# Sums of squares of the head norms in portions between column tiles, and another order of three branch products

## The chip, the cores and the metric

One core of a Trainium2 chip runs the whole program. The metric is the device time of one execution in microseconds (us). A median of several runs is compared; lower is better.

## What is computed

Two transformer blocks over 256 tokens of width 1024, in float32. Block one mixes a stick-breaking attention and a gated linear attention, then a feed-forward. Block two, where the change lies, is cut here to what matters:

```python
xn = rms_norm_2(x, norm_mix)
q_nsa, kv_nsa, g_nsa, conv_in, q_mem, g_merge = split(xn @ w_in)
q  = rms_norm_2(heads(q_nsa), qk_norm[0])              # 8 heads of 64
kc = rms_norm_2(compress_blocks(k_c, ...), qk_norm[1]) # gelu(blocks @ w1) @ w2
ks, kw = rms_norm_2(k_s, qk_norm[2]), rms_norm_2(k_w, qk_norm[3])   # 2 groups of 64
o_nsa  = nsa_attention(q, kc, vc, ks, vs, kw, vw, sigmoid(g_nsa))   # sparse attention
u      = silu(layer_norm(causal_conv(a * sigmoid(ag))))
qm     = rms_norm_2(q_mem, mem_qk_norm[0])             # 4 heads of 128
o_m    = softmax(qm @ km^T / sqrt(128)) @ vm           # attention to the memory
gm     = sigmoid(g_merge)                              # three gates of width 1024
merged = gm[0] * (o_nsa @ w_nsa_out) + gm[1] * (u @ w_conv_out) + gm[2] * (o_m @ w_mem_out)
h      = x + merged @ w_out
```

A feed-forward with a gate follows. The change alters no formula; only the order of the three terms of `merged` in their sum is another.

## The kernel before

Activations lie transposed: features on the 128 partitions, tokens along the row. Each weight matrix streams in as tiles of 128x1024 float32 (512 KB) on the queue of SP. `Stream.prepare` (L505 to L522) loads a tile into one of four `raw` buffers, casts it on ACT into one of three `hi` buffers (L520) and subtracts on DVE into one of three `lo` buffers (L522). A float32 product is made of three: hi times xh, hi times xl, lo times xh. In `gemm_b` these are L324, L326 and L328, eight matmuls of 128x256 each per column tile of 128 columns when the inner dimension is 1024; the first pair of column tiles of a matrix can run in an interleaved order, L308 to L310 (lead). `gemm_a` (L367) puts the tokens on the partitions instead.

In `block_two` a section written out by hand (from L1095, `manual_schedule` for TensorE alone) sets TensorE's order. ACT's, DVE's and POOL's orders come from a scheduler, which goes by the priorities and by the place where an instruction is written. Generators hand out the work: `heads` makes the column tiles of the queries and keys, `cmp` is `compress` (eight small products "chunks" L1229 that gather a block's frames, a fold L1239, a gelu, then L1258, L1266, L1272), `gates` makes the 24 column tiles of the merge gates, and `pre` is `nsa_operands`. Each `next` issues one step of a generator, and `fill(g, n)` issues n column tiles.

`nsa_operands` squares the keys `ksw`, the queries `q` and the memory's queries `qm` on ACT (L1310, tile `hsq`), and sums the squares over each head on TensorE with the 20 matmuls of L1313, in which the squares are the weights (128x128) and the right side has one or two columns. Each is two passes in the trace, so 40 instructions. DVE adds an epsilon (`hn_v`, L1319), `rsqrt_exp` (L1292 to L1296) makes the reciprocal root in ACT and DVE, and L1328 spreads the keys' norms. Here it is called at once, behind the fold L1239; L1117 (a small product for the head gates) and `gemm_a` (the values, L367) come next, and then L1258, which needs the gelu's result `cmp_h` (L1250). The sigmoid of the gelu is `cmp_t`: L1283 (DVE), L1284 (ACT), L1285 and L1286 (DVE).

Beyond the hand-written section TensorE's order is the scheduler's too. `branch(n)` multiplies a product by its gate (L1151, DVE) and adds into a running sum (L1153): `wmo` (memory) starts the sum, `wno` (sparse attention) is added on POOL, `wco` (convolution) on DVE; then `split` (ACT L426, DVE L427) makes the halves `mrg` that `wo2` reads first in its lead loop L308. In `before`, `wmo` comes first, while the last head of the memory attention (L1520) is still being made.

Of the kernel before, what the change touches and what calls it, by code (L numbers as in the profile page):

```python
# [13 lines left out]
OP = mybir.AluOpType  # L14
# [423 lines left out]
def fill(steps, n):  # L438
    for _ in range(n):
        next(steps, None)  # L440


def finish(steps):
    for _ in steps:
        pass
# [597 lines left out]
def block_two(K, B, KM, vm, out):  # L1043
    nc, tc, a, par, con = K.nc, K.tc, K.a, K.par, K.con
# [5 lines left out]
    ON, OM = Halves(K, "on", 4), Halves(K, "om", 4)  # L1050
    gm = [K.t4("gm") for _ in range(6)]
    cv = K.t4("cv")
    kc2 = [K.small("PT", [128, 384], bufs=4)[:, :256].rearrange("p (g t) -> p g t", g=2) for _ in range(2)]
    N = Bag()
# [43 lines left out]
    with tc.manual_schedule(engines={mybir.EngineType.PE}):  # L1098
        heads = K.steps_b(_Shift(st, 64), 8, 12, B.X, evb)
        fill(heads, 6)  # L1100
        cmp = compress(K, kc2, N)
        for _ in range(6):
            next(cmp)
            fill(heads, 1)
        next(cmp)
        pn = K.gemm_n(K.narrow("wgn", B.gain), B.x)
        with tc.high_priority(offset=50000):
            nc.vector.tensor_tensor(gn, pn, rr, op=OP.mult)
        next(cmp)
        gates = K.steps_b(K.stream("w2g"), 8, 24, B.X, evg)  # L1110
        fill(gates, 2)
        next(cmp)
        pre = nsa_operands(K, N, B.eps)
        next(pre)
        pg = K.pt()[:, :48].rearrange("p (t n) -> p t n", t=2)
        for t in range(2):
            mm(pg[:, t], lhsT=gn[:, t * 128:t * 128 + 128], rhs=con["fold"][:, :24], start=True, stop=True)  # L1117
        N.gate = K.small("gate", [128, 2, 24], bufs=1)
        with tc.issue_after(s3.ins):
            nc.scalar.preload_act_table_set("natural_log_exp_and_others")  # L1120
            sigmoid(K, N.gate, pg)

        K.gemm_a(K.stream("w2v", 256), 8, 1, B.X, 256, evv)
        next(cmp)
        finish(pre)
        fill(gates, 1)
        finish(cmp)
        with tc.issue_after(s3.ins):
            last = nsa(K, N, ON, mem_attention(K, N, KM, vm, OM), gates)
        finish(gates)  # L1130
# [16 lines left out]
    def branch(n):  # L1147
        def ev(i, c, ps):
            d = slice((i % 4) * 256, (i % 4 + c) * 256)
            g_, t = gm[2 * n + i // 4][:, d], gm[4 + i // 4][:, d]  # L1150
            nc.vector.tensor_tensor(g_, ps.rearrange("p a t -> p (a t)"), g_, op=OP.mult)  # L1151
            if n != 2:
                (nc.vector if n == 1 else nc.gpsimd).tensor_tensor(t, t, g_, op=OP.add)  # L1153
            if n == 1:
                K.split(M.h(i, c), M.l(i, c), t)
        return ev

    K.gemm_b(K.stream("wmo"), 4, 8, OM, branch(2))
    K.gemm_b(K.stream("wno"), 4, 8, ON, branch(0))
    K.gemm_b(K.stream("wco"), 4, 8, UC, branch(1), single=2)  # L1160
    XF = Halves(K, "xf", 8)
    sqs = Squares(K)
# [118 lines left out]
def sigmoid(K, out, x, scale=1.0):  # L1281

    K.nc.vector.tensor_scalar(out, x, -87.0 / scale, None, op0=OP.max)  # L1283
    K.nc.scalar.activation(out, out, AF.Exp, scale=-scale)  # L1284
    K.nc.vector.tensor_scalar(out, out, 1.0, None, op0=OP.add)  # L1285
    K.nc.vector.reciprocal(out, out)  # L1286


def rsqrt_exp(K, v, y, t):

    nc = K.nc
    nc.scalar.activation(t, v, AF.Ln)  # L1292
    nc.scalar.activation(y, t, AF.Exp, scale=-0.5)
    nc.vector.tensor_tensor(t, y, y, op=OP.mult)
    nc.vector.scalar_tensor_tensor(t, t, -0.5, v, op0=OP.mult, op1=OP.mult)
    nc.vector.scalar_tensor_tensor(y, t, 1.5, y, op0=OP.add, op1=OP.mult)  # L1296
    return y


def nsa_operands(K, N, eps):  # L1300

    nc, par, con = K.nc, K.par, K.con
    mm = nc.tensor.matmul
    q, ksw = N.q, N.ksw
    sums = K.pt()[:, :32].rearrange("p (t n) -> p t n", t=2)
    at = 0
    for x, n, rhs, m in ((ksw, 2, con["mean64"][:, ::64], 2), (q, 4, con["mean64"][:, ::64], 2),
                         (N.qm, 4, con["one128"], 1)):
        sq = K.t4("hsq")[:, :n * 256]
        nc.scalar.activation(sq, x, AF.Square)  # L1310
        for t in range(2):
            for i in range(n):
                mm(sums[:, t, at + i * m:at + i * m + m], lhsT=sq[:, i * 256 + t * 128:i * 256 + t * 128 + 128],  # L1313
                   rhs=rhs, start=True, stop=True)
        at += n * m
    v, y, w = (K.small(n, [128, 32], bufs=1) for n in ("hn_v", "hn_y", "hn_w"))
    y3 = y.rearrange("p (t n) -> p t n", t=2)
    for t in range(2):
        nc.vector.tensor_scalar(v[:, t * 16:t * 16 + 16], sums[:, t], eps[:, t:t + 1], None, op0=OP.add)  # L1319
    rsqrt_exp(K, v, y, w)  # L1320
    rk, N.rq, N.rqm = y3[:, :, :4], y3[:, :, 4:12], y3[:, :, 12:]
    yield
    pk = K.pt()
    for j in range(2):
        for g in range(2):
            for t in range(2):
                o = j * 256 + t * 128
                mm(pk[g * 64:g * 64 + 64, o:o + 128], lhsT=rk[:, t, 2 * j + g:2 * j + g + 1].to_broadcast([128, 64]),  # L1328
                   rhs=K.ident, start=True, stop=True)
    KK = ksw.rearrange("p (j t) -> p j t", j=2)  # L1330
    for j in range(2):
        nc.vector.scalar_tensor_tensor(KK[:, j], ksw[:, j * 256:j * 256 + 256], K.gain_k[:, 1 + j:2 + j],
                                       pk[:, j * 256:j * 256 + 256], op0=OP.mult, op1=OP.mult)


    N.qs = [K.t4("qs", F32R) for _ in range(2)]
    N.kh, N.kl = (K.t4("ks", F32R).rearrange("p (g n) -> p g n", g=2) for _ in range(2))
    for g in range(2):
        own, far = slice(g * 64, g * 64 + 64), slice(64 - g * 64, 128 - g * 64)
        nc.scalar.copy(N.qs[g][own], q[own])  # L1340
        nc.vector.tensor_tensor(N.qs[g][far], q[own], N.qs[g][own].bitcast(F32), op=OP.subtract)
        nc.scalar.copy(N.kh[own, g], ksw[own])
        nc.vector.tensor_tensor(N.kl[own, g], ksw[own], N.kh[own, g].bitcast(F32), op=OP.subtract)
        nc.scalar.copy(N.kh[far, g], ksw[own])
        nc.scalar.copy(N.kl[far, g], N.kl[own, g].bitcast(F32))
# [144 lines left out]
def mem_attention(K, N, KM, vm, OM):  # L1490
    nc = K.nc
    mm = nc.tensor.matmul
    qm, rq = N.qm, N.rqm

    def head(h):
        hs = slice(h * 256, h * 256 + 256)
        ps = K.pt().rearrange("p (t m) -> p t m", t=2)
        for t in range(2):
            mm(ps[:, t], lhsT=qm[:, h * 256 + t * 128:h * 256 + t * 128 + 128], rhs=KM[:, hs], start=True, stop=True)
        mx, den = K.small("mxm", [128, 2], bufs=2), K.small("denm", [128, 2], bufs=2)  # L1500
        nc.vector.tensor_reduce(mx, ps, axis=mybir.AxisListType.X, op=OP.max)
        nc.vector.scalar_tensor_tensor(mx, mx, -1.0, rq[:, :, h], op0=OP.mult, op1=OP.mult)
        P = K.small("P1", [128, 2, 256], bufs=4)
        for t in range(2):
            N.last = nc.scalar.activation(P[:, t], ps[:, t], AF.Exp, scale=rq[:, t, h:h + 1], bias=mx[:, t:t + 1],
                                          accum_out=den[:, t:t + 1])
        nc.vector.reciprocal(den, den)
        for t in range(2):
            nc.vector.tensor_scalar(P[:, t], P[:, t], den[:, t:t + 1], None, op0=OP.mult)
        yield  # L1510
        pt = K.pt().rearrange("p (m t) -> p m t", m=2)
        for t in range(2):
            for m in range(2):
                nc.tensor.transpose(pt[:, m, t * 128:t * 128 + 128], P[:, t, m * 128:m * 128 + 128], K.ident)
        PT = K.small("PTm", [128, 512], bufs=1).rearrange("p (m t) -> p m t", m=2)
        nc.scalar.copy(PT, pt)
        yield
        po = K.pt("pc")[:, :256]
        for m in range(2):
            mm(po, lhsT=vm[:, m * 512 + h * 128:m * 512 + h * 128 + 128], rhs=PT[:, m], start=m == 0, stop=m == 1)  # L1520
        K.split(OM.h(h), OM.l(h), po)

    return head
# [84 lines left out]
```

## Time and profile before

| what | value |
|---|---|
| runs, us | 918.21, 918.55, 919.99 (median 918.55) |
| profiled execution, us | 920.02, of which the trace's span 918.2 |
| TensorE matmul (PE) | 900.6 us busy, 98% of the span |
| TensorE weight loads (PEld) | 828.4 us, 90% |
| DVE | 675.6 us, 74% |
| ACT | 491.1 us, 53% |
| POOL | 51.1 us, 6% |
| mean granted TensorE clock | 0.991 of full |

Busy time counts an instruction from its start to its modelled end; weight loads run beside matmuls. In the trace's views of one engine in order of time, a row merges consecutive instructions of one line: its start, its length, their number, and in brackets the idle time before it with the engine and line that ended it. The next row can start a little before the end of the one ahead, since matmuls are pipelined. In a view of stretches a row has the stretch, its length, the busy time (with the number of instructions) of PE, PEld, DVE, ACT and POOL or of the engine asked for, then the granted TensorE clock (1.00 is 2.4 GHz, 0.50 is 1.2 GHz), the DMA engines' share and GB/s.

### The profile page before, as it was taken

To read this page: it belongs to the slowest core of one execution; us is meant where nothing else is said; L and a number is where in the kernel's file an instruction comes from. 1 tells how busy PE (TensorE), PEld (TensorE's weight loads), DVE (VectorE), ACT (ScalarE), POOL (GpSimd) and SP (SyncE) were. 2 spreads that over 40 slices of the span, in tenths; PEclk is the share of its full clock that TensorE was granted. 3 is DMA by queue.
4 is the path that set the end of the run, shared out by engine and by line. 5 is a ranking of instruction groups with operands and counts; after the bars stand their busy time and mean duration, and the time that the engine had idled before them with its cause. 6 is when DMAs were issued, how large, how long until landed. Compare 5 with 4: busy or idle time off the path is not lost.

```text
span 918.2 us, 17035 instructions
## 1 busy us (share of the span) xinstructions
PE 900.6 (98%) x6818; PEld 828.4 (90%) x6818; DVE 675.6 (74%) x1169; ACT 491.1 (53%) x747; POOL 51.1 (6%) x82
## 2 busy tenths in 40 slices
PE   8998999999999999999999999899999999999998
PEld 6987689999999999888899988799999988888887
DVE  6996768866677666555557986899988788888653
ACT  6653764654456555444444434667854565555432
POOL 1000001210020000001120000000003200000000
PEclk9999999999999999999999998999999999999999
DMA  7643426765666666555656762343445566666672
GB/s 274 202 138 117 115 70 184 228 196 174 195 194 196 180 185 186 173 173 185 189 165 186 225 224 75 95 136 118 116 135 164 184 189 186 191 189 185 193 204 64
DMA packets 45727, 155.64 MB, mean 170 GB/s; under 512 B 5200, under 2 KB 6736, under 8 KB 45648
## 3 DMA queue, kind: packets, MB, share of 16 engines
q1 hardware_dynamic: 45216, 153.48, 54.7%
q8 instruction: 53, 0.87, 0.4%
q10 hardware_dynamic: 432, 1.08, 0.4%
q14 instruction: 26, 0.21, 0.1%
HBM read 153.49 MB, written 1.05 MB: 168 GB/s over the span
## 4 chain that ended last, share of the span: by engine, by line
PE 94%; DVE 3%; issue 1%; ACT 1%; DMA 0%; SPq 0%; DVEq 0%
PE pj L295 18%; PE pj L324 17%; PE pj L326 16%; PE pj L328 16%; PE pj L296 9%; PE pj L367 6%; DVE lo L522 1%; PE pj L309 1%; PE pj L310 1%; PE pj L308 1%; ACT hi L520 1%; PE pt L913 1%; PE pt L1313 1%; PE pt L403 1%; PE pt L1229 1%
## 5 line engine op out<-in xcount | busy, mean ns | idle before, releaser
L520 ACT CAST hi<-raw 128x1024 fp32r<-128x1024 f32 (+1 forms) x278 | 288.6, 1041 | 315.7 <-PE pj L326 133.7
L522 DVE TENSOR_TENSOR lo<-raw,hi 128x1024 fp32r<-128x1024 f32 (+1 forms) x278 | 341.3, 1230 | 105.4 <-ACT hi L520 93.4
L295 PE MATMUL pj<-hid,hi 128*128 128x512 f32 x378 | 134.3, 400 | 0.0
L295 PE MATMUL pj<-xf,hi 128*128 128x512 f32 x320 | 113.2, 399 | 0.0
L296 PE MATMUL pj<-hid,lo 128*128 128x256 f32 x378 | 106.2, 281 | 0.0
L296 PE MATMUL pj<-xf,lo 128*128 128x256 f32 x320 | 89.8, 281 | 0.0
L295 PEld LDWEIGHTS pj<-hid,hi 128*128 128x128 f32 x378 | 71.0, 188 | 17.4
L295 PEld LDWEIGHTS pj<-xf,hi 128*128 128x128 f32 x320 | 60.1, 188 | 14.9
L296 PEld LDWEIGHTS pj<-hid,lo 128*128 128x128 f32 x378 | 71.4, 189 | 0.0
L296 PEld LDWEIGHTS pj<-xf,lo 128*128 128x128 f32 x320 | 60.4, 189 | 0.0
L1536 DVE SCALAR_TENSOR_TENSOR cv<-u,par,cv 128x256 f32<-128x256 f32 x120 | 53.2, 479 | 0.7
L324 PE MATMUL pj<-xm,hi 128*128 128x256 f32 x336 | 50.9, 294 | 0.0
L324 PEld LDWEIGHTS pj<-xm,hi 128*128 128x128 f32 x336 | 44.2, 193 | 5.0 <-ACT hi L520 2.5
L326 PE MATMUL pj<-xm,hi 128*128 128x256 f32 x336 | 47.9, 286 | 0.0
L328 PE MATMUL pj<-xm,lo 128*128 128x256 f32 x336 | 47.2, 283 | 0.0
L328 PE MATMUL pj<-xn,lo 128*128 128x256 f32 x304 | 44.8, 286 | 0.0
L469 POOL TENSOR_TENSOR acc<-acc,ffr 128x256 f32<-128x256 f32 (+1 forms) x25 | 27.3, 1103 | 310.4 <-ACT ffr L462 288.9
L326 PEld LDWEIGHTS pj<-xm,hi 128*128 128x128 f32 x336 | 44.1, 195 | 0.0
L326 PE MATMUL pj<-xn,hi 128*128 128x256 f32 x304 | 44.0, 285 | 0.0
L324 PE MATMUL pj<-xn,hi 128*128 128x256 f32 x304 | 43.8, 285 | 0.0
L328 PEld LDWEIGHTS pj<-xm,lo 128*128 128x128 f32 x336 | 43.5, 193 | 0.0
L328 PEld LDWEIGHTS pj<-xn,lo 128*128 128x128 f32 x304 | 39.7, 192 | 0.5 <-issue 0.4
(471 smaller groups left out, 1632.0 us busy)
## 6 DMA issues: line engine op xcount, KB each, us to landing
raw<-in_wf_dram SPq DMA_DIRECT2D x64, 512.0 KB, 3.7
raw<-in_wgu_dram SPq DMA_DIRECT2D x44, 512.0 KB, 3.7
raw<-in_w1g_dram SPq DMA_DIRECT2D x24, 512.0 KB, 3.8
raw<-in_w2g_dram SPq DMA_DIRECT2D x24, 512.0 KB, 3.7
raw<-in_wdn_dram SPq DMA_DIRECT2D x22, 512.0 KB, 3.9
raw<-in_w2a_dram SPq DMA_DIRECT2D x20, 512.0 KB, 3.7
raw<-in_wo_dram SPq DMA_DIRECT2D x16, 512.0 KB, 3.8
raw<-in_w1a_dram SPq DMA_DIRECT2D x14, 512.0 KB, 3.8
```

Source lines behind the costliest of these rows:

```text
L295: mm(ps, lhsT=st.hi(w), rhs=x.both(k), start=k == 0, stop=False, skip_group_check=True)
L296: mm(ps[:, :T], lhsT=st.lo(w), rhs=x.h(k), start=False, stop=k == kt - 1, skip_group_check=True)
L308: mm(ps[:, j], lhsT=st.hi(w), rhs=x.h(k), start=k + j == 0, stop=False, skip_group_check=True)
L309: mm(ps[:, j], lhsT=st.hi(w), rhs=x.l(k), start=False, stop=False, skip_group_check=True)
L324: mm(ps[:, j], lhsT=st.hi(o + k), rhs=x.h(k), start=k == 0, stop=False)
L326: mm(ps[:, j], lhsT=st.hi(o + k), rhs=x.l(k), start=False, stop=False)
L328: mm(ps[:, j], lhsT=st.lo(o + k), rhs=x.h(k), start=False, stop=k == kt - 1)
L367: mm(pss[t], lhsT=xx(k)[:, t * 128:t * 128 + 128], rhs=ww(o + k), start=k == 0 and xx == x.h and ww == st.hi, stop=k == kt - 1 and ww == s ...
L469: self.engine.tensor_tensor(a, a, s, op=OP.add)
L520: nc.scalar.copy(hi[:, o:o + n], raw[:, o:o + n])
L522: nc.vector.tensor_tensor(lo[:, o:o + n], raw[:, o:o + n], hi[:, o:o + n].bitcast(F32), op=OP.subtract)
L1536: nc.vector.scalar_tensor_tensor(o, u[:, c, k:k + 256], w[:, c, k:k + 1], o, op0=OP.mult, op1=OP.add)
```

## The change

Sums of squares: `nsa_operands` is made earlier and yields four more times. Its sums for `ksw` are issued in one portion behind the second chunk of `compress`, those for `q` in two (one for each half of the tokens) behind the fourth and the sixth, the first half of `qm` between the first two column tiles of the gates, the second half behind the fold. Branches: `wno` comes before `wmo`, the sum runs in the first two of the six gate tiles `gm`, and all adds are on DVE.

```diff
--- before.py
+++ after.py
@@ -1099,8 +1099,12 @@
         heads = K.steps_b(_Shift(st, 64), 8, 12, B.X, evb)
         fill(heads, 6)
         cmp = compress(K, kc2, N)
-        for _ in range(6):
+        pre = nsa_operands(K, N, B.eps)
+        for i in range(6):
             next(cmp)
+
+            if i in (1, 3, 5):
+                next(pre)
             fill(heads, 1)
         next(cmp)
         pn = K.gemm_n(K.narrow("wgn", B.gain), B.x)
@@ -1108,9 +1112,10 @@
             nc.vector.tensor_tensor(gn, pn, rr, op=OP.mult)
         next(cmp)
         gates = K.steps_b(K.stream("w2g"), 8, 24, B.X, evg)
-        fill(gates, 2)
+        fill(gates, 1)
+        next(pre)
+        fill(gates, 1)
         next(cmp)
-        pre = nsa_operands(K, N, B.eps)
         next(pre)
         pg = K.pt()[:, :48].rearrange("p (t n) -> p t n", t=2)
         for t in range(2):
@@ -1147,16 +1152,16 @@
     def branch(n):
         def ev(i, c, ps):
             d = slice((i % 4) * 256, (i % 4 + c) * 256)
-            g_, t = gm[2 * n + i // 4][:, d], gm[4 + i // 4][:, d]
+            g_, t = gm[2 * n + i // 4][:, d], gm[i // 4][:, d]
             nc.vector.tensor_tensor(g_, ps.rearrange("p a t -> p (a t)"), g_, op=OP.mult)
-            if n != 2:
-                (nc.vector if n == 1 else nc.gpsimd).tensor_tensor(t, t, g_, op=OP.add)
+            if n:
+                nc.vector.tensor_tensor(t, t, g_, op=OP.add)
             if n == 1:
                 K.split(M.h(i, c), M.l(i, c), t)
         return ev
 
+    K.gemm_b(K.stream("wno"), 4, 8, ON, branch(0))
     K.gemm_b(K.stream("wmo"), 4, 8, OM, branch(2))
-    K.gemm_b(K.stream("wno"), 4, 8, ON, branch(0))
     K.gemm_b(K.stream("wco"), 4, 8, UC, branch(1), single=2)
     XF = Halves(K, "xf", 8)
     sqs = Squares(K)
@@ -1312,7 +1317,11 @@
             for i in range(n):
                 mm(sums[:, t, at + i * m:at + i * m + m], lhsT=sq[:, i * 256 + t * 128:i * 256 + t * 128 + 128],
                    rhs=rhs, start=True, stop=True)
+            if n == 4 and t == 0:
+                yield
         at += n * m
+        if at < 16:
+            yield
     v, y, w = (K.small(n, [128, 32], bufs=1) for n in ("hn_v", "hn_y", "hn_w"))
     y3 = y.rearrange("p (t n) -> p t n", t=2)
     for t in range(2):
```

Behind the diff all lines are up to 9 further on: L1313 is L1318, L1239 is L1244, L1117 is L1122, L1229 is L1234, L1151 is L1156, L1153 is L1158, L1292 is L1297, L1284 is L1289, L1520 is L1529.

TensorE at the end of the hand-written stretch of heads and gates (`hsq` holds squares, `con` the constant columns, `P` the chunks' sums, `xm` the activations), before:

```order
L328 MATMUL pj_6042<-xm_4415,lo_6076 128x256 x2
L1239 MATMUL pt_6104<-con,P_874_6040 128x2x15 x4
L1313 MATMUL pt_6120<-con,hsq_6121 128x2 x4
L1313 MATMUL pt_6120<-con,hsq_6127 128x2 x8
L1313 MATMUL pt_6120<-con,hsq_6137 128x1 x8
L1117 MATMUL pt_6157<-con,glow_5255 128x24 x2
L367 MATMUL pj_6166<-hi_6170,xm_4412 128x256
```


and with the change:

```order
L328 MATMUL pj_6059<-xm_4414,lo_6099 128x256 x2
L328 MATMUL pj_6059<-xm_4415,lo_6099 128x256 x2
L1244 MATMUL pt_6127<-con,P_877_6057 128x2x15 x4
L1318 MATMUL pt_5816<-con,hsq_6090 128x1 x4
L1122 MATMUL pt_6157<-con,glow_5255 128x24 x2
L367 MATMUL pj_6166<-hi_6170,xm_4412 128x256
```


Sixteen of the 20 matmuls have left this place, for places among the column tiles ahead.

ACT at the same place (`hi` and `raw` are weight tiles, `cmp_t` belongs to the gelu, `hn_*` to the head norms), before:

```order
L520 CAST hi_6200<-raw_6198 128x1024
L520 CAST hi_6280<-raw_6278 128x1024
L520 CAST hi_6325<-raw_6323 128x1024
L1292 ACTIVATE hn_w_6149<-hn_v_6147 128x32
L1284 ACTIVATE gate_6160<-gate_6160 128x48
L1284 ACTIVATE cmp_t_6111<-cmp_t_6111 128x128
L1293 ACTIVATE hn_y_6148<-hn_w_6149 128x32
L520 CAST hi_6384<-raw_6382 128x1024
```


and with the change:

```order
L520 CAST hi_6200<-raw_6198 128x1024
L520 CAST hi_6280<-raw_6278 128x1024
L1297 ACTIVATE hn_w_6149<-hn_v_6147 128x32
L1298 ACTIVATE hn_y_6148<-hn_w_6149 128x32
L1289 ACTIVATE gate_6160<-gate_6160 128x48
L1289 ACTIVATE cmp_t_6134<-cmp_t_6134 128x128
L520 CAST hi_6325<-raw_6323 128x1024
L520 CAST hi_6384<-raw_6382 128x1024
```


The cast of one weight tile (`hi_6325`) moves from ahead of the four small functions to behind them, and L1293 (now L1298) ahead of the two L1284 (now L1289).

DVE among the branch products (`pj` is a product, `gm` the gates and the sums, `uc` and `cv` the convolution), before:

```order
L1151 TENSOR_TENSOR gm_5244<-pj_7789,gm_5244 128x512
L1151 TENSOR_TENSOR gm_5244<-pj_7822,gm_5244 128x512
L1151 TENSOR_TENSOR gm_5245<-pj_7855,gm_5245 128x512
L522 TENSOR_TENSOR lo_7960<-raw_7957,hi_7959 128x1024
L1151 TENSOR_TENSOR gm_5245<-pj_7888,gm_5245 128x512
L522 TENSOR_TENSOR lo_7995<-raw_7992,hi_7994 128x1024
L1151 TENSOR_TENSOR gm_5246<-pj_7921,gm_5246 128x512
L522 TENSOR_TENSOR lo_8030<-raw_8027,hi_8029 128x1024
L1153 TENSOR_TENSOR gm_5248<-gm_5248,gm_5246 128x512
L1151 TENSOR_TENSOR gm_5246<-pj_7956,gm_5246 128x512
L522 TENSOR_TENSOR lo_8074<-raw_8071,hi_8073 128x1024
L427 TENSOR_TENSOR mrg_7657<-gm_5248,mrg_7657 128x2x256
```


and with the change:

```order
L1156 TENSOR_TENSOR gm_5248<-pj_7789,gm_5248 128x512
L522 TENSOR_TENSOR lo_7960<-raw_7957,hi_7959 128x1024
L1158 TENSOR_TENSOR gm_5244<-gm_5244,gm_5248 128x512
L1156 TENSOR_TENSOR gm_5248<-pj_7822,gm_5248 128x512
L1156 TENSOR_TENSOR gm_5249<-pj_7855,gm_5249 128x512
L522 TENSOR_TENSOR lo_7995<-raw_7992,hi_7994 128x1024
L1158 TENSOR_TENSOR gm_5244<-gm_5244,gm_5248 128x512
L1158 TENSOR_TENSOR gm_5245<-gm_5245,gm_5249 128x512
L1156 TENSOR_TENSOR gm_5249<-pj_7888,gm_5249 128x512
L522 TENSOR_TENSOR lo_8030<-raw_8027,hi_8029 128x1024
L1158 TENSOR_TENSOR gm_5245<-gm_5245,gm_5249 128x512
L1156 TENSOR_TENSOR gm_5246<-pj_7921,gm_5246 128x512
```


Adds of 128x512 that stood in POOL's list (four, L1153) now stand in DVE's, between the products' L1156 and the weights' L522; the instructions of TensorE are as many as before, POOL has four fewer, and the four loads of `wno` stand ahead of those of `wmo` on SP.

## Rows read from the trace of the kernel before

**Rows 1.** the page's parts 1 (busy time) and 4 (engines of the chain)

```profile
PE 900.6 (98%) x6818; PEld 828.4 (90%) x6818; DVE 675.6 (74%) x1169; ACT 491.1 (53%) x747; POOL 51.1 (6%) x82
...
PE 94%; DVE 3%; issue 1%; ACT 1%; DMA 0%; SPq 0%; DVEq 0%
```

**Rows 2.** stretches of block two: length, busy of each engine, then TensorE clock, DMA

```profile
520.60:546.20 25.60, 25.60 (x236) 22.16 (x233) 25.50 (x50) 12.07 (x14) 0.00 (x0) 1.00 0.81 255
...
546.00:549.56 3.56, 3.56 (x35) 3.56 (x34) 2.63 (x5) 0.49 (x1) 0.00 (x0) 1.00 0.55 147
...
549.56:559.76 10.20, 10.20 (x49) 10.20 (x49) 2.13 (x10) 1.63 (x5) 0.00 (x0) 0.50 0.14 51
...
580.25:583.67 3.42, 3.42 (x18) 3.42 (x18) 1.87 (x8) 0.80 (x4) 0.00 (x0) 0.50 0.09 32
```

**Rows 3.** TensorE in order of time: start, length, line, x instructions [idle before]

```profile
527.27 0.64 PE L1229 MATMUL pt<-P,P 128*32 128x256 f32 x8
...
546.20 0.97 PE L1239 MATMUL pt<-con,P 128*128 128x30 f32 x8
...
547.01 6.38 PE L1313 MATMUL pt<-con,hsq 128*128 128x2 f32 x40
...
553.25 1.03 PE L1117 MATMUL pt<-con,glow 128*128 128x24 f32 x4
...
554.10 3.76 PE L367 MATMUL pj<-hi,xm 128*128 128x256 f32 x16
...
564.59 0.42 PE L1258 MATMUL pt<-cmp_h,par 128*64 128x16 f32 x8 [2.02 <-DVE hn_y L1296]
```

**Rows 4.** TensorE on L1313 alone, before and after the clock fell

```profile
547.01:549.56 2.55, 2.55 (x23) 1.00 0.42 164
...
549.56:553.25 3.69, 3.69 (x19) 0.50 0.38 142
```

**Rows 5.** ACT in order of time around the wait on TensorE

```profile
557.90 1.04 ACT L520 CAST hi<-raw 128x1024 fp32r<-128x1024 f32 x1 [11.41 <-PE pj L367]
...
559.12 0.30 ACT L1284 ACTIVATE cmp_t<-cmp_t 128x128 f32<-128x128 f32 x1
```

**Rows 6.** DVE in order of time, same place

```profile
563.02 1.22 DVE L522 TENSOR_TENSOR lo<-raw,hi 128x1024 fp32r<-128x1024 f32 x1 [0.54 <-ACT hi L520]
...
564.16 0.28 DVE L1250 TENSOR_TENSOR cmp_h<-cmp_h,cmp_t 128x128 f32<-128x128 f32 x1
```

**Rows 7.** TensorE in order of time, block one's head norms

```profile
382.52 1.95 PE L1034 MATMUL pt<-con,hsq 128*128 128x1 f32 x16
```

**Rows 8.** the stretch of block one that holds them

```profile
380.00:386.00 6.00, 6.00 (x40) 5.33 (x39) 2.52 (x10) 3.52 (x5) 0.00 (x0) 1.00 0.59 170
```

**Rows 9.** ACT's squares: length min/median/max in ns, first and last start in us

```profile
L1310 ACT ACTIVATE hsq<-q x1: 1062/1062/1062, 524.4 to 524.4; 128x1024 f32<-128x1024 f32 x1
...
L1310 ACT ACTIVATE hsq<-qm x1: 1061/1061/1061, 538.9 to 538.9; 128x1024 f32<-128x1024 f32 x1
```

**Rows 10.** TensorE in order of time, the scores after the memory heads

```profile
577.00 0.85 PE L1400 MATMUL pt<-ks,qs 128*128 128x256 f32 x3 [0.70 <-ACT ks L1345]
```

**Rows 11.** TensorE in order of time, the branch products

```profile
667.46 1.10 PE L1520 MATMUL pt<-PTm,vm 128*128 128x256 f32 x4 [0.84 <-DVE om L427]
...
669.02 0.38 PE L324 MATMUL pj<-om,hi 128*128 128x256 f32 x1 [0.46 <-ACT om L426]
...
703.85 0.28 PE L308 MATMUL pj<-mrg,hi 128*128 128x256 f32 x1
```

**Rows 12.** DVE in order of time, the branch sums

```profile
693.14 2.15 DVE L522 TENSOR_TENSOR lo<-raw,hi 128x1024 fp32r<-128x1024 f32 x1
...
697.46 0.68 DVE L1153 TENSOR_TENSOR gm<-gm,gm 128x512 f32<-128x512 f32 x1
...
700.03 0.68 DVE L427 TENSOR_TENSOR mrg<-gm,mrg 128x512 fp32r<-128x512 f32 x1
```

**Rows 13.** POOL in order of time, the branch sums

```profile
689.41 7.04 POOL L1153 TENSOR_TENSOR gm<-gm,gm 128x512 f32<-128x512 f32 x4 [212.18 <-DVE gm L1151]
```

## The prediction

> **What bounds the kernel now.** I read the page first, then the granted clock by stretches, then each engine in order of time around every place where TensorE is slow or waits. The page shows TensorE busy for 98% of the span and 94% of the chain that ended last, with DVE 3% and ACT 1% [rows 1]. So the time is TensorE's: what shortens it must either give TensorE less to do, let it run faster, or take away one of its few waits. DVE at 74% as a mean says little, because it is nearly full in some stages (25.50 of 25.60 us in the heads' stage [rows 2]).
>
> The clock by stretches shows where TensorE runs slowly. In the stage of the heads and the first gates, 520.60 to 546.20, it is at 1.00. It stays there to 549.56, and then stands at 0.50 for 10.20 us; a second such stretch, 3.42 us, comes at 580.25 [rows 2]. TensorE was busy without a gap ahead of the first fall (3.56 of 3.56 us [rows 2]). What it did there: after the dense column tiles, 0.97 us of the fold L1239 and then the 40 instructions L1313 with a right side of one or two columns [rows 3]. So a long run of very narrow products goes ahead of the fall; L1313 goes on in it, and L1117 and most of `gemm_a` L367 pay for it. Behind `gemm_a` TensorE waits 2.02 us for the gelu's result before L1258 [rows 3]. The view of waits puts that down to `hn_y`, but L1258 reads `cmp_h`, made at 564.16 and just ahead of it on DVE [rows 6].
>
> **The change, part by part.** All sums are against the profiled execution, 920.02 us, which is 1.47 above the median of 918.55.
>
> *The clock.* 32 of the 40 narrow instructions go elsewhere. At full clock one takes 2.55/23 = 0.111 us, at half clock 3.69/19 = 0.194 [rows 4]; where they go they cost 0.111 each, as in their first half now, so their number itself costs and saves nothing. If the clock stays up, the 3.69 us of them at half clock become 3.69 x 0.111/0.194 = 2.1 (-1.6), and the other 10.20 - 3.69 = 6.51 us, which are L1117 and L367, become half (-3.25). That is -4.8. The ends: 0, if the clock falls all the same, and half of 10.20, -5.1. I take -4.8, because the longest row of narrow products that is left (fold about 0.8, last portion 8 x 0.111 = 0.9, L1117 about 0.4) is 2.1 us, against some 0.8 + 2.55 = 3.4 us before the fall now. The nearest row with another outcome is block one's own head norm: 16 instructions of one column, 1.95 us, dense work on both sides [rows 7], and the clock there is 1.00 [rows 8]. The 2.1 us lie close to it, but not under it; that stays in the range.
>
> The Trainium skill, page "TensorE: Matmul & The Clock Gate", section "Why this matters for your kernels", names idle gaps between bursts of matmuls as what brings the clock down. The row above speaks against it here, since TensorE was busy throughout. Taken by its word the narrow products would be innocent and spreading them would save none of the 4.8 us; that is a rival below.
>
> *The wait before L1258.* ACT sat idle for 11.41 us until a buffer came free from L367, with a weight cast (L520, 557.90) at the head of its queue, and only behind it came `cmp_t` at 559.12 [rows 5]. On DVE two weight subtractions stand between that and L1250: one ahead of the reciprocals, and a second, 1.22 us at 563.02, right ahead of L1250 at 564.16 [rows 6]. With the change that cast stands behind `cmp_t` on ACT, and only one L522 stands between the reciprocals and L1250. By my count from the start s of L367: DVE needs about 1.2 us past it for the inputs of `cmp_t`, ACT 0.3 [rows 5], DVE about 2.3 for its small work up to both reciprocals, 1.2 for the one L522 and 0.2 for L1250 [rows 6], which is s + 5.2. L367 itself is 48 instructions at half of 3.76/16 [rows 3], 0.12, so s + 5.8. So the wait goes, -2.0, with half a us to spare; the ends are 0 (another late cast) and -2.02. What is late next is ACT: a cast now stands between two `ks` copies, and TensorE already waits 0.70 for `ks` at 577.00 [rows 10]. I add 0.3; its ends are 0 and one cast, 1.04 [rows 5]. The portions' inputs cost nothing: the squares of `q` are made by 524.4 + 1.06 and those of `qm` by 538.9 + 1.06 [rows 9], while their first portions come behind the chunk of 527.27 [rows 3] and behind the first gate tile, some 3 us ahead of the fold at 546.20 [rows 3]; ACT's work for them does not change.
>
> *The branches.* TensorE waits 0.84 us for a copy of `om` before the last memory head's L1520 and 0.46 before the first product after it [rows 11], since `wmo` needs that head. With `wno` first, the head and the two small products of the convolution's norm lie under 15 us of other products: -1.3 and about 0.6 more in lags around them, so TensorE would reach `wo2` at about 701.9 in place of 703.85 [rows 11]. But DVE gives `mrg`, and it gets more to do: four adds of 128x512 at 0.6 to 0.68 [rows 12], 2.4 in all, less what it regains. While POOL ran its four adds, 7.04 us [rows 13], the worst of three L522 took 2.15 in place of 1.22 [rows 6, 12], 0.9 over, and the two others about half of that together. So DVE has about 1.0 more, ahead of a `mrg` that was written at 700.03 and after [rows 12]. By hand, instruction by instruction, the second half of `mrg` is ready about 1.15 after TensorE wants it, the lead loop ends 0.66 earlier than now. I take -0.7; the ends are -1.95 (DVE keeps up) and +1.5 (DVE is late by all its adds less the part that was idle). The four loads of `wno` ahead of those of `wmo` on SP cost nothing: as many tiles go through the same four buffers, and the loop is not waiting for them.
>
> *The second slow stretch* costs half of 3.42, 1.7 [rows 2]. It follows waits and narrow scores and can stay, go or shift; I leave it in the sum as it is and put it into the range.
>
> The sum: -4.8 - 2.0 + 0.3 - 0.7 = -7.2, so 912.8 for an execution like the profiled one, and 911.4 for one like the median. I put the forecast at 912.0, between them and nearer to the second.
>
> **Rivals.**
>
> *A spell of half clock is left.* The 2.1 us of narrow products at the end bring the clock down once, for a stretch like the second one: +1.7, 913.7. For it: block one's run that stayed up was 1.95 [rows 7], which is no longer than this. Against it: ahead of it stand 5.8 us of dense tiles.
>
> *DVE ends the branches.* TensorE waits for `mrg` for as long as DVE's adds are late: +1.5 where I have -0.7, so 914.2. For it: DVE is the fuller engine there, and its L522 also feeds TensorE. Against it: POOL's slowing goes.
>
> *The narrow products are not the cause* (the change does not do what it seems to). The clock then falls around L1117 and L367 all the same, and only the wait and the branches are won: -2.0 + 0.3 - 0.7 = -2.4, 917.6 profiled, about 916.6 as a median. For it: one single stretch shows the link. Against it: TensorE was busy without a gap before the fall [rows 2].
>
> *Slower.* The portions bring the clock down in the stage that is now at 1.00 [rows 2]. Each second step there would have a chunk of 0.64 [rows 3] and a portion of 0.9 next to only 24 x 0.12 = 2.9 us of dense tile. It decides once more than 7.2 us of full-speed work run at half speed; if the clock fell with the second portion of `q` and stayed down to the fold, some 12 us of work would take 24, and the time would be 912.8 + 12 = 924.8. Against it: a chunk is a 128x256 product, and the run of 1.95 us [rows 7] left the clock alone.
>
> **How the numbers follow.** Forecast 0.64, the left-over spell 0.17, DVE 0.08, innocent narrow products 0.06, slower 0.04, and 0.01 for the rest. The range, 909.3 to 915.5, takes in the forecast with its ends (second stretch gone, -1.7, and DVE keeping up, -1.2, together about 909.1), the left-over spell and the late DVE, and both of these at once short of a few tenths. A measurement of this kernel can tell about 0.2%, 1.84 us, from no change, so "same" is 916.7 to 920.4: half of the innocent case and a few mishaps lie there. Faster 0.90, same 0.06, slower 0.04.
>
> **What would show it.** In the profile after: clock 1.00 from the fold to the end of L367, the narrow products at 0.111 each in five places, L367 in about 5.9 us, no wait before L1258; L1529 without a wait in front, a short wait or none at L308, and L522 at 1.22 among the branches. A clock of 0.50 anywhere between 520 and 562 would prove the first step wrong; a wait of over 0.5 us before L1258 the second; a wait of over 2 us at L308 the fourth.

## The result, and the profile after

The changed kernel took 912.48 us (median of 4 runs, 910.81 to 913.59) against 919.13 before (4 runs, the three shown above and one more); the ratio is 0.9926 with a 95% interval of 0.9904 to 0.9948. That is 0.7% less time, and the forecast of 912.0 was inside. The profiled execution's span fell from 918.2 to 911.8.

The page's parts 1 and 4 of the changed kernel:

```profile
PE 896.4 (98%) x6818; PEld 825.3 (91%) x6818; DVE 676.5 (74%) x1173; ACT 491.2 (54%) x747; POOL 44.0 (5%) x78
...
PE 93%; DVE 4%; ACT 1%; issue 1%; DMA 0%; SPq 0%; DVEq 0%; ACTq 0%
```

TensorE's busy time is 4.2 us less [rows 1] at as many instructions, POOL's is 7.1 us less, which are the four adds [rows 13].

Its stretches, with the columns of [rows 2]:

```profile
520.30:549.29 28.99, 28.99 (x269) 25.68 (x265) 26.75 (x52) 12.08 (x14) 0.00 (x0) 1.00 0.71 231
549.29:551.44 2.15, 2.15 (x23) 2.15 (x21) 1.83 (x3) 0.29 (x1) 0.00 (x0) 1.00 0.47 187
551.44:557.38 5.94, 5.94 (x51) 5.81 (x50) 5.83 (x21) 2.80 (x6) 0.00 (x0) 1.00 0.38 98
572.40:579.30 6.90, 6.90 (x34) 6.90 (x34) 2.49 (x12) 3.32 (x11) 0.00 (x0) 0.51 0.17 64
```

The heads with three portions and the first gates run at 1.00, and so do the fold with the last portion (2.15 us) and the values' product (5.94 us). The 10.20 us at half clock [rows 2] are gone. But the second slow stretch, 3.42 us before, is 6.90 us long.

TensorE in order of time:

```profile
536.67 1.05 PE L1318 MATMUL pt<-con,hsq 128*128 128x2 f32 x8
...
549.29 0.97 PE L1244 MATMUL pt<-con,P 128*128 128x30 f32 x8
550.10 1.03 PE L1318 MATMUL pt<-con,hsq 128*128 128x1 f32 x8
...
551.44 2.17 PE L367 MATMUL pj<-hi,xm 128*128 128x256 f32 x16
...
557.38 0.42 PE L1263 MATMUL pt<-cmp_h,par 128*64 128x16 f32 x8
...
569.79 0.85 PE L1409 MATMUL pt<-ks,qs 128*128 128x256 f32 x3 [0.70 <-ACT ks L1354]
571.52 2.71 PE L1375 MATMUL pt<-cmp_kn,q 128*128 128x32 f32 x16 [0.88 <-DVE nb L1420]
...
581.59 0.55 PE L1439 MATMUL pt<-con,P 128*128 128x128 f32 x3 [1.78 <-DVE P L1429]
```

There is no wait in front of L1263, where L1258 waited 2.02 us [rows 3]. The wait for the key copies, 0.70, is as before [rows 10]; those before the compressed scores and behind the scores have grown, from 0.46 to 0.88 and from 1.56 (0.44 and 1.12) to 1.78. TensorE before the compressed scores in the kernel before:

```profile
578.31 1.94 PE L1366 MATMUL pt<-cmp_kn,q 128*128 128x32 f32 x16 [0.46 <-DVE nb L1411]
```

The view puts this wait down to `nb`, but L1366 and L1375 read `cmp_kn`. In both kernels DVE makes that soon behind a weight subtraction, and ends it some 0.15 us ahead of the product. DVE with the change:

```profile
569.56 1.22 DVE L522 TENSOR_TENSOR lo<-raw,hi 128x1024 fp32r<-128x1024 f32 x1
...
571.19 0.18 DVE L1283 TENSOR_TENSOR cmp_kn<-cmp_k,con 128x32 f32<-128x32 f32 x1
```

To see where the time went I put the starts of the same instructions side by side:

| instruction | before, us | after, us | shift |
|---|---|---|---|
| chunk ahead of the first portion | 520.00 | 519.79 | -0.21 |
| compressed keys, L1258 / L1263 | 564.59 | 557.38 | -7.21 |
| second scores, last three, L1400 / L1409 | 577.00 | 569.79 | -7.21 |
| compressed scores, L1366 / L1375 | 578.31 | 571.52 | -6.79 |
| next head's scores, L1400 / L1409 | 587.12 | 581.89 | -5.23 |
| first branch product, L324 | 665.48 | 660.25 | -5.23 |
| first product of `wo2`, L308 | 703.85 | 696.88 | -6.97 |
| its third column tile, L326 | 710.57 | 704.20 | -6.37 |
| last product | 913.66 | 907.29 | -6.37 |

So the heads' place gives 7.0 us, the first scores take 2.0 back, the branches give 1.7, and the start of `wo2` takes 0.6. The 0.2 of the first row lie ahead of the first portion and belong to none of them.

### The profile page after: what moved, and what is told of

Its sections match the earlier page's. It is cut to its first block, busy times and chain, and to the rows that moved or that the text cites. A ratio compares the mean times of both kernels' runs of the same rounds, so it can differ in the third digit from the quotient of the medians.

```text
span 911.8 us, 17028 instructions
## 1 busy us (share of the span) xinstructions
PE 896.4 (98%) x6818; PEld 825.3 (91%) x6818; DVE 676.5 (74%) x1173; ACT 491.2 (54%) x747; POOL 44.0 (5%) x78
## 4 chain that ended last, share of the span: by engine, by line
PE 93%; DVE 4%; ACT 1%; issue 1%; DMA 0%; SPq 0%; DVEq 0%; ACTq 0%
PE pj L295 18%; PE pj L324 16%; PE pj L326 16%; PE pj L328 16%; PE pj L296 9%; PE pj L367 6%; DVE lo L522 2%; PE pj L309 1%; PE pj L310 1%; PE pj L308 1%; ACT hi L520 1%; PE pt L913 1%; PE pt L403 1%; PE pt L1318 1%; DMA raw<-in_w1a_dram 0%
## 5 line engine op out<-in xcount | busy, mean ns | idle before, releaser
L522 DVE TENSOR_TENSOR lo<-raw,hi 128x1024 fp32r<-128x1024 f32 (+1 forms) x278 | 339.7, 1224 | 104.1 <-ACT hi L520 96.2
L295 PE MATMUL pj<-hid,hi 128*128 128x512 f32 x378 | 134.2, 399 | 0.0
L295 PE MATMUL pj<-xf,hi 128*128 128x512 f32 x320 | 113.2, 399 | 0.0
L295 PEld LDWEIGHTS pj<-hid,hi 128*128 128x128 f32 x378 | 71.0, 188 | 17.3
L295 PEld LDWEIGHTS pj<-xf,hi 128*128 128x128 f32 x320 | 60.1, 188 | 14.8
L324 PE MATMUL pj<-xm,hi 128*128 128x256 f32 x336 | 51.1, 294 | 0.0
L326 PE MATMUL pj<-xm,hi 128*128 128x256 f32 x336 | 47.9, 286 | 0.0
L324 PEld LDWEIGHTS pj<-xm,hi 128*128 128x128 f32 x336 | 44.4, 193 | 3.8 <-issue 1.9
L326 PEld LDWEIGHTS pj<-xm,hi 128*128 128x128 f32 x336 | 44.1, 195 | 0.0
L326 PE MATMUL pj<-xn,hi 128*128 128x256 f32 x304 | 44.0, 285 | 0.0
L324 PE MATMUL pj<-xn,hi 128*128 128x256 f32 x304 | 43.8, 285 | 0.0
```

What stands on the lines that cost most here:

```text
L295: mm(ps, lhsT=st.hi(w), rhs=x.both(k), start=k == 0, stop=False, skip_group_check=True)
L324: mm(ps[:, j], lhsT=st.hi(o + k), rhs=x.h(k), start=k == 0, stop=False)
L326: mm(ps[:, j], lhsT=st.hi(o + k), rhs=x.l(k), start=False, stop=False)
L522: nc.vector.tensor_tensor(lo[:, o:o + n], raw[:, o:o + n], hi[:, o:o + n].bitcast(F32), op=OP.subtract)
```

## The experiments

Runs of one kernel lay further apart than I had taken: before took 914.55 to 919.48 us in one series of 17 runs and 912.82 to 919.80 in another of 11. Some of that is in parts that the kernels share. The ratios lie near those of the mean times, so they need not be the quotients of the medians. So beside the medians I use a length inside each profile, from the start of the fold (128x30) to the first joint product L295 of the last feed-forward. It leaves out the portions ahead of the fold: 32 x 0.111 = 3.6 us, by which before and kernels with its lump are longer here for no loss.

| kernel | fold to L295, us | of it at 0.50, us |
|---|---|---|
| before | 186.8 (183.3 without 3.6) | 10.2 + 3.4 |
| changed | 177.4 | 6.8 |
| changed, second profile (after_again) | 175.8 | 3.4 |
| portions_only | 176.9 | 3.4 |
| branches_only | 187.2 (183.7) | 10.2 + 3.4 + 3.4 |
| adds_on_pool | 177.1 | 6.8 |
| gelu_ahead | 184.6 (181.1) | 6.8 + 3.4 |
| cover | 172.7 | 0 |
| cover_pool | 172.6 | 0 |

**One part of the change at a time.** portions_only is the changed kernel with the branches taken back, as shown here; branches_only is the kernel before with the same lines edited the other way:

```diff
-            g_, t = gm[2 * n + i // 4][:, d], gm[i // 4][:, d]
+            g_, t = gm[2 * n + i // 4][:, d], gm[4 + i // 4][:, d]
-            if n:
-                nc.vector.tensor_tensor(t, t, g_, op=OP.add)
+            if n != 2:
+                (nc.vector if n == 1 else nc.gpsimd).tensor_tensor(t, t, g_, op=OP.add)
-    K.gemm_b(K.stream("wno"), 4, 8, ON, branch(0))
     K.gemm_b(K.stream("wmo"), 4, 8, OM, branch(2))
+    K.gemm_b(K.stream("wno"), 4, 8, ON, branch(0))
```

> The change with the branches as they were before (order, gate tiles and POOL adds). Theory A (the gain comes from the narrow products' place): by the two traces the heads' place gives 7.0 us (clock 4.7, the wait before the compressed keys 2.0, small gaps 0.3) and the stretch of first scores takes 2.0 back, so about 5.1 us faster than before, some 914; clock at 1.00 from the fold to the end of the values' product. Theory B (the branches carry the gain): within 2 us of before.

> The kernel before with the three edits of the branches alone. Theory A: the heads' place is as before (clock at 0.50 for about 10 us, a wait of 2.0 us), and the branches give about 1.1 us, of which TensorE reaches the output product 1.7 us earlier and loses 0.6 there: some 918. Theory B: 4 us or more faster.

portions_only: 911.78 us against 917.72, ratio 0.9953 (0.9934 to 0.9971). branches_only: 916.96, ratio 1.0001 (0.9986 to 1.0017). The portions carry the gain; the branches' 1.1 us, 0.9988 as a ratio, lie inside what the runs can tell. The lengths tell more: between portions_only and after_again, both with one slow stretch of 3.4 us, the branches give 1.1 us. Between before and branches_only they give 1.3, if half of the latter's additional 3.4 us is taken off. TensorE in portions_only:

```profile
556.14 0.42 PE L1263 MATMUL pt<-cmp_h,par 128*64 128x16 f32 x8
...
659.44 1.10 PE L1529 MATMUL pt<-PTm,vm 128*128 128x256 f32 x4 [0.84 <-DVE om L427]
661.00 0.38 PE L324 MATMUL pj<-om,hi 128*128 128x256 f32 x1 [0.46 <-ACT om L426]
```

and in branches_only:

```profile
561.34 0.42 PE L1258 MATMUL pt<-cmp_h,par 128*64 128x16 f32 x8 [2.02 <-DVE hn_y L1296]
...
665.75 1.10 PE L1520 MATMUL pt<-PTm,vm 128*128 128x256 f32 x4
...
703.19 0.39 PE L309 MATMUL pj<-mrg,hi 128*128 128x256 f32 x1 [0.32 <-DVE mrg L427]
```

Each has the waits of the part that it lacks, and not those of the part that it has: 2.02 before the compressed keys with the lump, 0.84 and 0.46 at the memory's last head with the old order. The new order of the branches brings its own wait for `mrg`, 0.32.

**The adds.** adds_on_pool is the changed kernel with `wmo`'s four adds on POOL:

```diff
             if n:
-                nc.vector.tensor_tensor(t, t, g_, op=OP.add)
+                (nc.vector if n == 1 else nc.gpsimd).tensor_tensor(t, t, g_, op=OP.add)
```

> The changed kernel with its new branch order, but the four 128x512 adds of the memory's branch on POOL again. Theory A (the adds on DVE make the output product's first halves late): the 0.6 us lost there in the changed kernel go, 0.6 us faster than it. Theory B (POOL's adds lengthen DVE's weight subtractions by as much as they take off DVE): no difference, and the subtractions next to POOL's adds take 1.4 us or more in place of 1.22.

910.36 us, ratio 0.9925 (0.9902 to 0.9947), by runs no different from the change. POOL and DVE in its trace:

```profile
683.38 7.86 POOL L1158 TENSOR_TENSOR gm<-gm,gm 128x512 f32<-128x512 f32 x4 [206.62 <-DVE gm L1156]
```

```profile
686.05 1.79 DVE L522 TENSOR_TENSOR lo<-raw,hi 128x1024 fp32r<-128x1024 f32 x1
...
690.00 1.78 DVE L1158 TENSOR_TENSOR gm<-gm,gm 128x512 f32<-128x512 f32 x1
```

Both theories were half right. DVE's operations next to POOL's adds take longer (L522 1.79, an L1158 1.78 in place of 0.68), and still `wo2` comes better off: from its first product to L326 of the third tile take 7.02 us, 7.32 with the adds on DVE and 6.72 before. That is 0.3, not 0.6.

**What brings the clock down.** All three start from the changed kernel. extra_narrow puts 20 products of two columns into the stage of dense tiles; extra_wide the same weights with 128 columns (`junk[:, :128]`, `rhs=K.ident`). Neither's sums are read. qm_together puts the last two portions together behind the fold. extra_narrow:

```diff
             if i in (1, 3, 5):
                 next(pre)
+            if i == 4:
+                junk = K.pt()
+                for r in range(20):
+                    mm(junk[:, :2], lhsT=ksw[:, (r % 4) * 128:(r % 4) * 128 + 128],
+                       rhs=con["mean64"][:, ::64], start=True, stop=True)
```

and qm_together:

```diff
-        fill(gates, 1)
-        next(pre)
-        fill(gates, 1)
+        fill(gates, 2)
         next(cmp)
         next(pre)
+        next(pre)
```

> The changed kernel with 20 more products (40 instructions) of two columns behind the fifth chunk, in the stage of dense tiles where nothing waits; their sums are read by nobody. Theory A (a long run of narrow products brings the clock down by itself): the clock falls to 0.50 in or right behind them, and the time grows by more than their 4.4 us: by 6 to 10 us. Theory B (the fall needs waits or the place behind the fold): the clock stays at 1.00 and the time grows by 4.4 us or less.

> The same 20 products with 128 columns in place of two: the weights loaded are the same. Theory A (few columns per weight load are what brings the clock down): the clock stays at 1.00, and the time grows by about the products' own 4.5 to 5 us. Theory B (the weight loads or the plain products on activations do it): the clock falls as with two columns.

> The changed kernel with both portions of the memory queries behind the fold, so that 16 narrow products run in a row there: with the fold and the small gate product about 3.1 us without a dense product, against 2.15 in the changed kernel and 7.1 before. Theory A (the length of the narrow run decides): if that is long enough the clock falls for one stretch of 3 to 10 us, costing 1.7 to 5; if not it stays at 1.00 and the time is that of the changed kernel. Theory B (the fall comes from somewhere else, such as the values' product behind): no difference.

Stretches of extra_narrow, of extra_wide and of qm_together:

```profile
531.55:533.90 2.35, 2.35 (x25) 2.35 (x21) 2.35 (x5) 0.12 (x1) 0.00 (x0) 0.99 0.74 254
533.90:544.10 10.20, 10.20 (x53) 9.51 (x52) 1.81 (x5) 1.04 (x1) 0.00 (x0) 0.50 0.22 75
```

```profile
533.16:537.65 4.49, 4.49 (x44) 4.49 (x41) 4.49 (x11) 0.12 (x1) 0.00 (x0) 1.00 0.88 296
537.65:548.00 10.35, 10.35 (x106) 8.74 (x105) 9.24 (x20) 4.64 (x6) 0.00 (x0) 1.00 0.37 113
```

```profile
548.50:551.90 3.40, 3.40 (x33) 3.40 (x32) 3.22 (x9) 0.32 (x1) 0.00 (x0) 1.00 0.72 186
552.10:555.40 3.30, 3.30 (x17) 3.30 (x17) 2.77 (x11) 1.11 (x5) 0.00 (x0) 0.50 0.29 115
```

TensorE in extra_narrow, right behind the narrow products:

```profile
538.04 2.05 PE L324 MATMUL pj<-xm,hi 128*128 128x256 f32 x8
```

The narrow products alone reproduce the loss: 2.35 us into them the clock falls, for 10.20 us, in a stage where TensorE waits for nothing and is busy all along; and as before the dense tiles behind pay for it: the eight products at 538.04 take 2.05 us, 1.20 in extra_wide. The same 20 weight loads with 128 columns take 4.49 us and leave the clock at 1.00, in fact less than the narrow ones with their slow part (6.49 from 531.55 to 538.04). The times, one run each, say the same more weakly: 919.73 with narrow, 916.98 with wide products. So the rival of the innocent narrow products is ruled out. The number of columns is not all that differs between the two runs: the right side holds constants in one and an identity in the other. The Trainium skill, page "TensorE: Matmul & The Clock Gate", section "Why this matters for your kernels", names idle gaps; that does not cover this case, since TensorE was busy for 2.35 of 2.35 us ahead of the fall. In qm_together, one run of 913.66 us, the run of fold, two portions and L1121, some 3.0 us, is followed by 3.4 us at half clock, and L367 takes 7.42 us in place of 5.94. The changed kernel's 2.15 us were not followed by a fall, in any of the nine profiles that have this run; the lump of 40 was, in all four that have it.

**What made the 2.0 us wait.** Two edits of the kernel before keep the narrow lump and alter only who goes first on ACT, or on ACT and DVE. `N.gelu` is the gelu's exponential on ACT in cast_behind, and its last product on DVE (L1250) in gelu_ahead; what is issued after it on its engine comes behind it:

```diff
         finish(pre)
-        fill(gates, 1)
+        with tc.issue_after(N.gelu.ins):
+            fill(gates, 1)
         finish(cmp)
```

and, in gelu_ahead alone, at the start of the work in `nsa`:

```diff
-    fill(gates, 1)
+    with K.tc.issue_after(N.gelu.ins):
+        fill(gates, 1)
     first(0)
```

> The kernel before, with the casts of the next gate tiles queued on ACT behind the gelu's exponential; TensorE's order is as before. Theory A (the wait of 2.0 us comes from a cast that stands ahead of the gelu on ACT and itself waits for a buffer): the wait before the compressed keys goes, the clock falls to 0.50 at the narrow products as before, and the time is about 2 us less. Theory B (the wait comes from the slow clock): it stays at 1.5 us or more.

> The kernel before, with the weight casts and subtractions of the next gate tiles queued behind the gelu on ACT and on DVE; TensorE's order is as before. Theory A (the wait of 2.0 us comes from the subtraction that stands right ahead of the gelu's last product on DVE and needs a cast that itself waits for a buffer of the values' product): the wait before the compressed keys goes, although the clock falls for 10 us as before; about 2 us less than before, some of it lost again if the gate tile's weights come late. Theory B (the slow clock makes the wait): it stays at about 2 us.

cast_behind: 919.28 us, one run; the casts stand behind the gelu on ACT, and the wait is 2.02 as before. TensorE, ACT and DVE in cast_behind (L1259 is L1258 of before, L1251 is L1250, L1287 the reciprocal):

```profile
563.90 0.42 PE L1259 MATMUL pt<-cmp_h,par 128*64 128x16 f32 x8 [2.02 <-DVE hn_y L1298]
```

```profile
560.96 1.05 ACT L520 CAST hi<-raw 128x1024 fp32r<-128x1024 f32 x1 [2.30 <-PE pj L367]
```

```profile
556.07 0.89 DVE L1287 RECIPROCAL cmp_t<-cmp_t 128x128 f32<-128x128 f32 x1
...
559.10 1.22 DVE L522 TENSOR_TENSOR lo<-raw,hi 128x1024 fp32r<-128x1024 f32 x1 [1.06 <-ACT hi L520]
562.33 1.23 DVE L522 TENSOR_TENSOR lo<-raw,hi 128x1024 fp32r<-128x1024 f32 x1 [2.00 <-ACT hi L520]
563.47 0.28 DVE L1251 TENSOR_TENSOR cmp_h<-cmp_h,cmp_t 128x128 f32<-128x128 f32 x1
```

The reciprocal is done at 556.96, but three weight subtractions stand ahead of L1251, and the last waits 2.00 us for a cast, which waits for a buffer that the values' product has not given back. In gelu_ahead L1251 stands ahead of them:

```profile
553.44 0.90 DVE L1287 RECIPROCAL cmp_t<-cmp_t 128x128 f32<-128x128 f32 x1
...
554.68 0.28 DVE L1251 TENSOR_TENSOR cmp_h<-cmp_h,cmp_t 128x128 f32<-128x128 f32 x1
554.88 2.59 DVE L522 TENSOR_TENSOR lo<-raw,hi 128x1024 fp32r<-128x1024 f32 x2
```

```profile
558.61 0.42 PE L1259 MATMUL pt<-cmp_h,par 128*64 128x16 f32 x8
...
568.19 0.85 PE L1401 MATMUL pt<-ks,qs 128*128 128x256 f32 x3 [1.44 <-ACT ks L1346]
```

The clock falls in it too (6.8 us), and there is no wait before L1259. So ACT's order alone leaves the wait as it is, and with DVE's order changed too it goes, though the clock falls: the weight subtractions ahead of L1251 on DVE made it. DVE's order was not changed by itself. The gate tile's late weights cost some of it again: the wait for `ks` is 1.44, and another of 2.63 comes up at 588 (915.54 us, one run; 2.2 us less from the fold to L295, of which the shorter slow stretch is 1.7).

**The second slow stretch.** cover moves a gate tile to the first scores; scores_behind puts the narrow compressed scores behind the tile that followed them; cover_pool is cover with the adds on POOL. cover, in `nsa` of the changed kernel:

```diff
     first(0)
-    fill(gates, 1)
+    fill(gates, 2)
     first(1)
```

and scores_behind:

```diff
     first(1)
-    scores()
     fill(gates, 1)
+    scores()
```

> The changed kernel with one gate tile taken from the end of the hand-written list and put behind the first head's scores, where TensorE waits 0.70 us for the key copies and 0.88 us for the row maxima. Theory A (waits next to narrow score products bring on the second slow stretch, 6.9 us at 0.50): both waits and the slow stretch go, 3 to 5 us faster than the changed kernel, less what the tile is missed for later. Theory B (the 16 narrow products of the compressed scores alone bring it on): the slow stretch stays at 3.4 us or more, and the gain is 1.5 us at most. Theory C: the tile is missed at the end by as much as it covers: no difference.

> The changed kernel with the 16 narrow products of the compressed scores one gate tile later, so that a dense tile stands between them and TensorE's wait of 0.70 us for the key copies. Theory A (waits and narrow scores next to each other bring on the second slow stretch): the wait of 0.88 us goes and the slow stretch of 6.9 us is gone or halved, 2 to 4 us less than the changed kernel. Theory B (narrow scores suffice): a slow stretch of 3.4 us or more follows them.

> The changed kernel itself, to stand beside the next one on the same chip: about 0.9926 of before, and a slow stretch of 3.4 or 6.9 us at the first scores.

> The changed kernel with the gate tile moved behind the first head's scores and the four adds on POOL. Theory A (both gains add up): no slow stretch behind the heads, the output product's first stage 0.3 us shorter than with the adds on DVE; 4 to 5 us less than the changed kernel. Theory B (the tile's gain was one of run to run): within 1.5 us of the changed kernel.

cover: 907.30 us, ratio to before 0.9900 (0.9884 to 0.9917). after_again took 912.09 (910.62 to 912.54; ratio 0.9942, 0.9920 to 0.9964) and cover_pool, beside it, 907.16 (905.64 to 907.61; ratio 0.9889, 0.9866 to 0.9913): their runs do not overlap. Not all of that is the tile's. The two profiled executions lie 6.9 us apart, 3.2 of it in the length from the fold to L295; the rest is mostly half of a stretch of 6.8 us at half clock near 77 us, which cover_pool does not have. Stretches of cover_pool, and TensorE in cover:

```profile
540.00:600.00 60.00, 58.85 (x503) 56.16 (x503) 55.95 (x168) 38.67 (x84) 0.00 (x0) 1.00 0.41 128
```

```profile
572.78 1.87 PE L1375 MATMUL pt<-cmp_kn,q 128*128 128x32 f32 x16
...
586.95 0.41 PE L1396 MATMUL pt<-con,sc 128*128 128x128 f32 x2 [0.73 <-DVE sc L1391]
...
666.04 0.74 PE L324 MATMUL pj<-om,hi 128*128 128x256 f32 x4 [0.66 <-ACT hi L520]
```

The 16 narrow scores are there as before, 1.87 us, and the clock stays up: with dense tiles right ahead of them instead of waits they do no harm in these two profiles, so theory B does not hold. The mean granted clock agrees over the runs: 0.9987 in the 11 of cover and cover_pool, 0.9956 in the 16 of the changed kernel, after_again and adds_on_pool. But one run of adds_on_pool, 906.92 us, stood at 1.000 without the moved tile, so the stretch can also stay away by itself. The two waits of 0.70 and 0.88 are gone, and the one behind the scores is 0.29. The missing tile costs 0.66 at a branch product and 0.73 behind the scores. By the lengths cover has 4.7 us less than the changed kernel's first profile and 3.1 less than its second. In cover_pool the adds on POOL were to give 0.3 more at the start of `wo2`; it took 7.25 us against 7.32 in cover, so they gave 0.1. scores_behind, one run of 905.76 us, keeps a stretch of 3.4 us at half clock behind a new wait:

```profile
566.85 0.85 PE L1409 MATMUL pt<-ks,qs 128*128 128x256 f32 x3 [0.70 <-ACT ks L1354]
...
570.41 1.87 PE L1375 MATMUL pt<-cmp_kn,q 128*128 128x32 f32 x16
573.22 0.33 PE L1439 MATMUL pt<-con,P 128*128 128x128 f32 x1 [0.94 <-DVE P L1429]
```

Which part waits and which part narrow products have in this stretch it does not settle; its length from the fold to L295 is 174.4, 1.4 less than after_again.

## Why the prediction was right, and where not

*The clock, -4.8:* measured -4.7. The lump of L1313 took 6.24 us before, the five portions 4.46; L1117 0.85 and 0.45, L367 8.47 and 5.94. The cause, the run of narrow products, is shown by extra_narrow and extra_wide; the step that 2.1 us of them would pass held. What I set against the left-over spell was misread, though: one gate tile, 2.95 us, stands between the portion ahead and the fold, not 5.8 us of dense tiles.

*The wait before L1258, -2.0:* measured -2.0, but I gave the reason half right. I named ACT's cast and DVE's subtraction; cast_behind shows that the cast's place on ACT is worth nothing by itself, gelu_ahead that the wait goes when the subtractions on DVE give way too. In the changed kernel one subtraction is left between the reciprocals and L1255, the counterpart of L1250, as I had counted:

```profile
555.02 1.16 DVE L522 TENSOR_TENSOR lo<-raw,hi 128x1024 fp32r<-128x1024 f32 x1
556.10 0.28 DVE L1255 TENSOR_TENSOR cmp_h<-cmp_h,cmp_t 128x128 f32<-128x128 f32 x1
```

L1255 began 4.7 us behind the start of L367, where I had counted 5.0.

*The copies of `ks`, +0.3:* measured 0; the wait is 0.70 in both. What did come is 0.4 at the compressed keys, before the scores that read them: 0.87 to 0.89 in six profiles of kernels with the portions, where before waits 0.46. My sum has no term for it.

*The branches, -0.7:* measured -1.1. TensorE came 1.74 earlier to `wo2` (I had 1.95) and lost 0.60 there (I had 1.3). DVE in the changed kernel stood between:

```profile
695.99 0.68 DVE L427 TENSOR_TENSOR mrg<-gm,mrg 128x512 fp32r<-128x512 f32 x1
696.59 1.29 DVE L1158 TENSOR_TENSOR gm<-gm,gm 128x512 f32<-128x512 f32 x2
697.80 1.22 DVE L522 TENSOR_TENSOR lo<-raw,hi 128x1024 fp32r<-128x1024 f32 x1
698.93 1.29 DVE L427 TENSOR_TENSOR mrg<-gm,mrg 128x512 fp32r<-128x512 f32 x2
```

```profile
698.31 0.33 PE L308 MATMUL pj<-mrg,hi 128*128 128x256 f32 x1
698.49 0.87 PE L324 MATMUL pj<-mrg,hi 128*128 128x256 f32 x6
699.67 0.39 PE L309 MATMUL pj<-mrg,hi 128*128 128x256 f32 x1 [0.31 <-DVE mrg L427]
```

The second halves of `mrg` come at 698.93, behind a weight subtraction; TensorE fills the time with six products of the third column tile that I had not foreseen (the row of six at 698.49), and waits only 0.31.

*The second slow stretch, 0:* here the sum failed. I left it as it was and put its going or coming into the range; the first scores took 2.0 us back in this profile, 1.6 by 6.9 us at half clock in place of 3.4 and the waits behind it, and 0.4 by the wait for the compressed keys. In after_again the stretch was 3.4 again, so its length is a matter of the run.

*The whole:* by the starts, -7.00 + 1.98 - 1.14 = -6.16 against my -7.2. That 912.0 came so near 912.48 is in part luck: the 2.0 that I had not foreseen met 0.4 more from the branches, 0.3 in small gaps and the 0.3 for `ks` that was not needed, and I had put the forecast between the sum for the profile and that for the median. Two figures beside the sum were off: innocent narrow products give 916.2 as a median, 918.55 - 2.4, not 916.6, and the lower ends add up to 909.1, just under the range.

*What a measurement can tell:* I took 0.2%. The runs of before alone spread over 0.5 to 0.8%, so the branches' part could not be seen in times, only in traces.

## What to carry to other kernels

Products with one or two columns cost more than their own time when they stand in one long run: the dense work behind them pays too. Hand them out among dense tiles. A dense tile in place of a wait next to those that remain helped here too, in cover; which of the two brings the second stretch on stays open. And look for a wait's cause in the queue of the engine that makes the operand: here a weight subtraction for a later tile, waiting for a buffer, stood ahead of the one small product that TensorE needed.

## What was unexpected

The length of a stretch at half clock is not the same from run to run of one kernel: 6.9 us at the first scores in one profile of the changed kernel, 3.4 in the other, and the one at 77 to 84 us, in code that no kernel here touches, lasted 3.4 us in most profiles, 6.8 in after_again and was missing in cover_pool, branches_only, extra_narrow and scores_behind. Each costs about half its length (the changed kernel's two profiles differ by 3.4 us at half clock there and some 1.5 in length), and they are one source of the runs' spread: the runs of adds_on_pool go from 913.13 us at a mean clock of 0.994 to 906.92 at 1.000. And 20 products of 128 columns (4.49 us) ended sooner than 20 of two columns that brought the clock down (6.49 us), before what the dense tiles behind lost.
